# A hybrid decoder step on one core: the last down groups over 148 then 128 columns, the state turned ahead of the squares, a fourth feature place, forget sums in three steps, first queries on GpSimd's queue

## The chip, the core and the metric

The kernel runs on one core of a Trainium2 chip. Its engines are TensorE (PE in the profile; PEld are its weight loads), VectorE (DVE), ScalarE (ACT), GpSimd (POOL) and SyncE (SP); each works through its own instructions in order, and they wait for one another through semaphores. DMAs are issued from the queues of SP, ACT and POOL. The metric is the device time of one execution in microseconds (us).

## The reference

One step of a two-layer decoder over 1,024 prompt rows, 16 meta rows and 64 sample rows (8 requests of 8), 1,024 wide, in fp32. Layer 0 mixes by a recurrence in chunks (8 heads, a state C and a vector n), layer 1 by attention with forget values: 16 heads, scores shifted by cumulative sums of log-forget values. A SwiGLU feed-forward (2,816 wide) follows each.

```
h, state = mlstm_sequence(q, k, v, li, lf, state0, lead)     # layer 0
out = (rmsnorm(h) * sigmoid(og)) @ w_out
...
s = q @ k.T + ci[..., None] - ckT[:, :, None, :]             # layer 1; ci, ckT: cumsum(lf)
p = softmax(where(pos_k <= pi, s, -inf));  o = p @ v
out = (o * sigmoid(og)) @ w_out
...
x = x + (silu(rmsnorm(x) @ w_gate) * (rmsnorm(x) @ w_up)) @ w_down    # after each layer
y = rmsnorm(x) * g_final
```

Outputs are the rows `y`, the states after the step, and the new keys, values and log-forget values.

## The kernel before, in words

An fp32 product is made of three matmuls on parts: each operand is split into a high part (ACT, L255, L261 or L267) and a low part (DVE, L256, L262 or L268), and PE adds high·high, low·high and high·low (L193 to L195, or inside L1402 and L1739). The order of most instructions is set by the framework's scheduler, which also decides which pieces of on-chip memory are used again and so what waits for what; two stretches have PE's order written by hand. The stages, with the places that the change touches:

- **Layer 0, recurrence.** Nine chunks of rows. The 64 sample rows come first: `first_queries` (L1157) stores their queries to DRAM (`qwD`, from POOL) and loads them back in four DMAs into `q2` (L1165, names `qq<-qwD`). Each of the four loads fills one half of the partitions with one of two head groups. DVE copies them into cleared tiles `qms` (L1227; the clearing is POOL's, L1167), and PE multiplies them with the old states (L1232). Each chunk ends with sums of squares of its heads on DVE and ACT (L1258, L1261). After the last chunk `last_state` (L1045) copies the vector n (DVE, L1050, `nnP`), turns it on PE (L1052) and stores it. The output projection `unit` (L517 to L539, PE name `pops`) follows; `add_sq` (L328) keeps the sums of squares for the next norm, its adds on POOL (L347) or, where `late`, on DVE (L345).
- **Feed-forward.** Gate and up products L1402. Down products L1739 run over groups of the weight's rows, for both halves of the outputs in turn. Their feature tiles come from DRAM by POOL's queue (L1529, `hr<-hB…`) into three places, and each is split by ACT and DVE (L267, L268); a split starts the load of the tile three items later. In layer 0 (`each`) the norm of finished column blocks runs beneath the products: sums (L360), root on ACT (L363), a copy on ACT (L379), reciprocal and a diagonal on DVE (L369, L371), and PE spreads it (L378, `nps`).
- **Layer 1, values and forget sums.** Values are projected in column groups 3, 1, 2 (`tmps`). `forget` (L2147 on) turns the log-forget rows on PE (L2169), scans them on DVE (L2174, `cnB`), stores them (`cD`), turns them back on PE (L2178, `fgcq`) and copies them (L2179, `cqP`). Beside it DVE makes the samples' own sums (`ncn`, L2223).
- **Layer 1, attention.** `attend_sample` (PE's order by hand) goes through pages of cached keys and values and, between them, projects the output gates `ogb` (ACT L2139, stored by POOL as `og2D`, L2140). Its last part multiplies sample queries with the new keys; the queries stand in two cleared tiles `qmt`, which live in the pool `sk` and are filled by 16 DVE copies of 64x16 elements. Then `attend_prompt` loads, per pair of heads, queries and keys in high and low parts (SP, L2524: `qh`, `kh`, `kl`, `ql`), the forget sums `ncb` (L2525, 1 MB), the values `vr` (L2531, L2533) and gates (L2537). PE makes scores `sp` (L2605), DVE takes maxima (L2609), POOL subtracts masks (`nd`, L2575).
- **Layer 1, feed-forward and tail.** The second feed-forward ends in class `Tail`: in the last two of the down groups (z = 6, the second half of the outputs, four row blocks of 128, so twelve matmuls of 276 columns for each of four m) each m is added (DVE L1383), squared (ACT L1814) and summed (DVE L1815). PE turns the rows back (L1825), the sums give root and reciprocal (L1846, L1848, L1849), DVE and ACT write the scaled rows (L1860, L1858), and SP stores them in six DMAs (L1863).

Of the kernel before, what the change touches and what calls it, by code (L numbers as in the profile page):

```python
# [176 lines left out]
class Net:  # L177
# [292 lines left out]
    def mlp(self, H, raws, w, l, heads=None, cb=None):  # L470
# [5 lines left out]
        with self.pool(self.uid("nsp")) as sp, self.pool(self.uid("npp"), bufs=2, space=PSUM) as pn:  # L476
# [14 lines left out]
            with ExitStack() as c:  # L491
# [30 lines left out]
                def unit(t, m, x):  # L522
# [9 lines left out]
                    self.add_sq(H, t, m, sp, x, KT - 1 if t < 3 else KT - 3)  # L532
# [424 lines left out]
def recurrence(self, kp, rec, v, qkD, fill, gate):  # L957
# [12 lines left out]
    with ExitStack() as cr, self.pool("recAp", bufs=2, space=PSUM) as pp:  # L970
# [28 lines left out]
        with self.pool("rec2") as sets[2], self.pool("rec1", bufs=2) as rp, self.pool("rec3") as sets[0]:  # L999
# [8 lines left out]
            for i in range(1, NT):  # L1008
# [10 lines left out]
                self.chunk_out(i, R, rp, *args, den, ssq, g, exp=N2 and N2["exp"])  # L1019
                if i == NT - 1:  # L1020
                    self.last_state(C[i % 2], pp, rp)
# [134 lines left out]
@_add(Net)  # L1156
def first_queries(self, R, sp):  # L1157

    nc = self.nc
    qd = self.dram.tile([P, 4, NS], F32, name="qwD")  # L1160
    nc.gpsimd.dma_start(qd, R["qw"][:, :, :NS])
    q2 = R["q2"]
    for a in range(2):
        for z in range(2):
            nc.sync.dma_start(q2[a * 64 : a * 64 + 64, :, z, :], qd[z * 64 : z * 64 + 64])  # L1165
    for qm in R["qms"]:
        nc.gpsimd.memset(qm, 0.0)  # L1167
# [26 lines left out]
def chunk_out(self, i, R, rp, pp, kp, C, v, qkD, eD, wD, tm, den, ssq, f, sp=None, exp=None):  # L1194
# [57 lines left out]
    if exp:  # L1252
        exp()
    R["nps"] = nps
# [99 lines left out]
def ffn(self, H, l, weights, order, TA, pn, pair, each, early, end=None):  # L1354
# [14 lines left out]
    with self.pool(f"ffn{l}") as fp, self.pool(f"ffnp{l}", space=PSUM) as pp:  # L1369
# [3 lines left out]
        fs = [fs0[:, x * SL : x * SL + SL] for x in range(6)]  # L1373
        fs += [H[3][:, k] for k in range(4)] + [H[2][:, k] for k in range(KT)] + [H[3][:, k] for k in range(4, KT)]
# [148 lines left out]
        def h_load(y):  # L1523
            if y < len(items):
# [3 lines left out]
                hraw[y] = self.ny(f"hr{l}_{y}")[:, :m]  # L1528
                nc.gpsimd.dma_start(hraw[y], hB[h, rounds[z][1]][:, c[0] : c[-1] + 1])  # L1529

        def h_split(y):
# [4 lines left out]
            h_load(y + 3)  # L1536
# [83 lines left out]
        with fixed(E.DVE, E.Activation):  # L1620
# [90 lines left out]
            for i, (hs, z, c) in enumerate(seq):  # L1711
# [18 lines left out]
                for m, h in [(m, h) for h in hs for m in range(4)] if apart else [(m, h) for m in range(4) for h in hs]:  # L1730
# [13 lines left out]
                    if last:  # L1744
# [3 lines left out]
                        if z in whole:  # L1748
# [6 lines left out]
                            elif not each and hs == (1,) and z == 6:  # L1755
                                square(3, m)
# [30 lines left out]
            if each:  # L1787
                self.first_values(H, pp, pn, lambda: norm(1, 2))
            else:
                tail.finish()  # L1790


class Tail:


    def __init__(self, net, fp, bank, pn, place):
        self.net, self.fp, self.bank, self.pn = net, fp, bank, pn
# [3 lines left out]
        self.count = {2: 0, 3: 0}  # L1801

    def square(self, t, m):
        nc, H = self.net.nc, self.net.H
        a, b = max(TS[t][0], self.at), TS[t][1]
        src = H[:, m, a:b]
        o = slice(a - self.at, b - self.at)
        c = self.count[t]
        self.count[t] += 1
        if c == 0:  # L1810
            nc.scalar.activation(self.sum[:, o], src, AF.Square)
        else:
            x = self.tmp[c % 2][:, : b - a]
            nc.scalar.activation(x, src, AF.Square)  # L1814
            nc.vector.tensor_tensor(out=self.sum[:, o], in0=self.sum[:, o], in1=x, op=ALU.add)  # L1815

    def gains(self):
        net = self.net
        for k in range(4, KT):
# [3 lines left out]
    def turn(self, ps, x, k):  # L1823
        t0, t1 = TT[DONE[3][x]]
        self.net.nc.tensor.transpose(ps[x][:, k % 4 * P : k % 4 * P + P], self.net.H[:, k, t0:t1], self.net.ident)  # L1825

    def new(self):
        return self.pn.tile([P, 512], F32, name=self.net.uid("fin"), tag="n")

    def second(self):  # L1830
        self.hi = [self.bank("fin"), self.bank("fin"), self.new()]
        for x in range(3):
            for k in range(4, KT):
                self.turn(self.hi, x, k)

    def finish(self):
        net, fp = self.net, self.fp
        nc, O, H = net.nc, net.O, net.H
        gr = net.sq[:, :512]
        lo = [self.bank("fin") for _ in range(3)]  # L1840
        ps = self.new()
        for x, ks in ((0, (0, 1)), (1, (0, 1)), (0, (2,)), (1, (2,)), (2, (0, 1, 2)), (0, (3,))):
            for k in ks:
                self.turn(lo, x, k)
        for x in range(3):
            nc.tensor.matmul(ps[:, x : x + 1], self.sum[:, x * P : x * P + P], net.ones[:, :1], start=True, stop=True)  # L1846
        r = fp.tile([P, 2, 3], F32, name="tr")
        nc.scalar.activation(r[:, 0], ps[:, :3], AF.Sqrt, scale=1.0 / D, bias=net.eps)  # L1848
        nc.vector.reciprocal(r[:, 1], r[:, 0])  # L1849
        for x in (1, 2):  # L1850
            self.turn(lo, x, 3)
        for x, i in enumerate(DONE[3]):
            t0, t1 = TT[i]
            for g, z in enumerate((lo, self.hi)):
                o = H[:, 4 * g : 4 * g + 4, t0:t1]
                y, rr = z[x].rearrange("p (k n) -> p k n", k=4), r[:, 1, x : x + 1]
                if g:
                    nc.scalar.activation(o, y, AF.Copy, scale=rr)  # L1858
                else:
                    nc.vector.scalar_tensor_tensor(out=o, in0=y, scalar=rr, in1=gr.rearrange("p (k n) -> p k n", k=4),  # L1860
                                                   op0=ALU.mult, op1=ALU.mult)
                dst = O["y_prompt"][0, (i - 1) * P : i * P, g * 512 : g * 512 + 512]
                nc.sync.dma_start(dst.rearrange("p (k n) -> p k n", k=4), o)  # L1863
# [131 lines left out]
def phase_b(self, ys, w7, cb):  # L1995
# [11 lines left out]
    with self.pool("fb", bufs=2) as fp, self.pool("fbp", bufs=2, space=PSUM) as pp:  # L2007
# [19 lines left out]
        for c in (3, 1, 2):  # L2027
# [11 lines left out]
            if c == 1:  # L2039
                for _ in forget:  # L2040
                    pass
# [109 lines left out]
def forget(self, lf):  # L2151
    nc, I, O = self.nc, self.I, self.O
    with self.pool("fg") as fp, self.pool("fgp", bufs=1, space=PSUM) as pp:
# [21 lines left out]
        nc.gpsimd.dma_start(self.cD, cn)  # L2175
# [634 lines left out]
```

## Time and profile before

| | |
|---|---|
| median of 3 runs | 2877.62 us (2868.31 to 2879.89) |
| the profiled execution | 2877.98 us |
| span of its instructions | 2876.3 us |
| mean granted TensorE clock | 0.988 |
| PE busy | 2778.6 us, 97% of the span |
| DVE, ACT, POOL busy | 1779.4, 1166.3, 833.7 us |
| DMA, mean | 163 GB/s |

The profiled execution is 1.7 us longer than its span. A row of a timeline shows start, duration, engine, line, operation, out<-in, shapes and count (x), and in brackets how long the engine was idle before and what ended that. A row of the windows view shows, for a stretch, its length, each engine's busy time with its count, the granted clock (1.00 is full), the DMA engines' share and GB/s. A row of the waits view shows total us, number and longest wait.

### The profile page before, as it was taken

Reading aid. Unit: us, or ns where it says so; the run is one execution under the profiler, and the core shown is the slowest. Engines: PE = TensorE matmul, PEld = TensorE weight load, DVE = VectorE, ACT = ScalarE, POOL = GpSimd, SP = SyncE. Lnnn points to the kernel's source line nnn. Section 1 sums busy time; section 2 is a strip of 40 time slices with the busy share of each in tenths; the row PEclk is TensorE's granted clock in tenths of the full one; section 3 lists DMA queues with packets and bytes.
Section 4 is the critical chain, followed back from the end, with each engine's and each line's share of the span. In section 5 each row is a group of like instructions: output and inputs, shape, how many; then the busy total and the mean of one; then the engine's idle time right before and its main releaser. Section 6 shows DMA issues by size and latency. Waiting matters only on the chain. (4 is left out here: it accounts for less than half of the span.)

```text
span 2876.3 us, 60505 instructions
## 1 busy us (share of the span) xinstructions
PE 2778.6 (97%) x23608; PEld 2663.7 (93%) x23608; DVE 1779.4 (62%) x3933; ACT 1166.3 (41%) x2279; POOL 833.7 (29%) x1291
## 2 busy tenths in 40 slices
PE   7999999999999999999999998999999999999998
PEld 7998888999999999999999887777899999999998
DVE  5141566788887656563355542677468888875656
ACT  5232363333232233443344443777533322323345
POOL 3021233223233322124263201455322232332111
PEclk9999999999999999999999998999999999999999
DMA  6374537245555375545343685443424555526566
GB/s 197 104 212 126 144 117 258 80 131 168 176 165 159 104 232 174 188 149 158 131 165 136 221 303 186 152 139 126 146 70 125 175 163 170 166 91 223 184 193 219
DMA packets 429353, 469.45 MB, mean 163 GB/s; under 512 B 41054, under 2 KB 355546, under 8 KB 428042
## 3 DMA queue, kind: packets, MB, share of 16 engines
q1 hardware_dynamic: 380066, 317.04, 35.7%
q0 software_dynamic: 43472, 142.88, 15.1%
q10 hardware_dynamic: 5528, 5.65, 0.6%
q8 instruction: 186, 3.05, 0.4%
q14 instruction: 101, 0.83, 0.1%
HBM read 318.25 MB, written 147.21 MB: 162 GB/s over the span
## 5 line engine op out<-in xcount | busy, mean ns | idle before, releaser
L1402 PE MATMUL m<-xh,slot 128*128 128x276 f32 x2752 | 540.6, 290 | 1.8 <-ACT fs L1431 1.8
L1402 PEld LDWEIGHTS m<-xh,slot 128*128 128x128 f32 x2752 | 439.6, 188 | 3.7 <-ACT fs L1431 2.4
L1402 PE MATMUL m<-xl,slot 128*128 128x276 f32 x1376 | 397.1, 289 | 0.0
L1402 PEld LDWEIGHTS m<-xl,slot 128*128 128x128 f32 x1376 | 258.7, 188 | 0.0
L193 PE MATMUL tmps<-slot,xh 128*128 128x256 f32 (+2 forms) x864 | 243.8, 282 | 0.0
L194 PE MATMUL tmps<-slot,xh 128*128 128x256 f32 (+2 forms) x864 | 241.5, 280 | 0.0
L195 PE MATMUL tmps<-slot,xl 128*128 128x256 f32 (+2 forms) x864 | 241.4, 279 | 0.0
L268 DVE TENSOR_TENSOR slot<-slot,slot 128x1024 fp32r<-128x1024 f32 x124 | 163.0, 1315 | 60.7 <-ACT slot L267 59.0
L267 ACT CAST slot<-slot 128x1024 fp32r<-128x1024 f32 x124 | 129.5, 1045 | 125.4 <-PE m L1402 109.8
L194 PEld LDWEIGHTS tmps<-slot,xh 128*128 128x128 f32 (+1 forms) x864 | 160.0, 185 | 0.2
L195 PEld LDWEIGHTS tmps<-slot,xl 128*128 128x128 f32 (+1 forms) x864 | 159.4, 185 | 0.0
L193 PEld LDWEIGHTS tmps<-slot,xh 128*128 128x128 f32 (+1 forms) x864 | 159.2, 184 | 0.1
L193 PE MATMUL mmA<-xh,whi 128*128 128x384 f32 (+1 forms) x384 | 134.0, 349 | 1.1 <-ACT stg L732 1.0
L194 PE MATMUL mmA<-xl,whi 128*128 128x384 f32 (+1 forms) x384 | 126.9, 330 | 0.0
L195 PE MATMUL mmA<-xh,wlo 128*128 128x384 f32 (+1 forms) x384 | 126.8, 330 | 0.0
L268 DVE TENSOR_TENSOR slot<-vA,slot 128x1024 fp32r<-128x1024 f32 (+1 forms) x59 | 82.2, 1396 | 32.7 <-ACT slot L267 31.5
L268 DVE TENSOR_TENSOR slot<-Ht,slot 128x1024 fp32r<-128x1024 f32 (+1 forms) x59 | 82.0, 1392 | 32.7 <-ACT slot L267 31.6
L256 DVE TENSOR_TENSOR wlo<-wraw,whi 128x1024 fp32r<-128x1024 f32 (+1 forms) x32 | 38.9, 1225 | 101.7 <-ACT whi L255 76.3
L267 ACT CAST slot<-Ht 128x1024 fp32r<-128x1024 f32 (+1 forms) x59 | 60.8, 1036 | 95.6 <-PE m L1402 88.6
L267 ACT CAST slot<-vA 128x1024 fp32r<-128x1024 f32 (+1 forms) x59 | 60.8, 1035 | 95.5 <-PE m L1402 82.7
L1506 DVE TENSOR_TENSOR ws<-ws 128x128 f32<-128x128 f32 x264 | 93.8, 355 | 8.8
L2632 ACT ACTIVATE s<-s,nb 128x272 f32<-128x272 f32 (+7 forms) x126 | 98.9, 787 | 0.0
(770 smaller groups left out, 8699.9 us busy)
## 6 DMA issues: line engine op xcount, KB each, us to landing
ws<-in_w_down SPq DMA_DIRECT2D x176, 128.0 KB
sD<-ws SPq DMA_DIRECT2D x176, 128.0 KB
slot<-sD SPq DMA_DIRECT2D x40, 512.0 KB
slot<-in_w_gate_up SPq DMA_DIRECT2D x36, 512.0 KB
kp<-in_cache_k SPq DMA_DIRECT2D x32, 512.0 KB
vp<-in_cache_v SPq DMA_DIRECT2D x32, 512.0 KB
vA<-in_w_gate_up SPq DMA_DIRECT2D x26, 512.0 KB
Ht<-in_w_gate_up SPq DMA_DIRECT2D x26, 512.0 KB
```

The source lines that it names most:

```text
L193: mm(ps, sh, mh, start=first, stop=False)
L194: mm(ps, sh, ml, start=False, stop=False)
L195: mm(ps, sl, mh, start=False, stop=last)
L256: low = lambda: nc.vector.tensor_tensor(out=lo, in0=raw, in1=hi.bitcast(F32), op=ALU.subtract)
L267: self.nc.scalar.copy(hi, src)
L268: self.nc.vector.tensor_tensor(out=lo, in0=src, in1=hi.bitcast(F32), op=ALU.subtract)
L1402: nc.tensor.matmul(u.ps[h, b], w[p][:, k], x[q][:, k], start=first and k == i == 0, stop=k == 3 and i == 2, skip_group_check=True)
L1506: tt(out=o, in0=a, in1=b, op=ALU.subtract)
L2632: nc.scalar.activation(ss[z, u], ss[z, u], AF.Exp, bias=nb[:, z : z + 1], accum_out=sm[:, u, z : z + 1])
```

## The change

It has seven parts.

1. The third block of the output projection (t = 2, both layers) makes the adds of two sums of squares on DVE and no more on POOL.
2. `last_state` runs between the copies of the last chunk's results and its sums of squares.
3. The four loads of the first queries go through POOL's queue and no more through SP's.
4. In layer 0's down products every fourth feature tile from item 11 on goes to a fourth place, the unused part of the tile `fs0`, and loads are issued four items ahead.
5. `forget` stops once more: turn and scan run at column group 1, the turning back at column group 2.
6. The two `qmt` tiles become one shared name in `attend_sample`'s own pool, cleared and filled by GpSimd (memset and copies). `sk`, which the memory behind comes after, is 4 KB a partition smaller.
7. The last two down groups leave the loop. `finish` makes them per m, first over the 148 columns that hold row tiles 6 and 7, then over the last 128; turning, root, scaling and stores of tiles 6 and 7 stand between the products of the last 128 columns.

```diff
-                    self.add_sq(H, t, m, sp, x, KT - 1 if t < 3 else KT - 3)
+                    self.add_sq(H, t, m, sp, x, KT - 1 if t < 2 else KT - 3)
...
-                if i == NT - 1:
-                    self.last_state(C[i % 2], pp, rp)
+                               then=(lambda: self.last_state(C[i % 2], pp, rp)) if i == NT - 1 else None)
...
-            nc.sync.dma_start(q2[a * 64 : a * 64 + 64, :, z, :], qd[z * 64 : z * 64 + 64])
+            nc.gpsimd.dma_start(q2[a * 64 : a * 64 + 64, :, z, :], qd[z * 64 : z * 64 + 64])
...
+        spare = fs0[:, 1024 : 1024 + 2 * SL].rearrange("p (k n) -> p k n", k=2)
-                hraw[y] = self.ny(f"hr{l}_{y}")[:, :m]
+                hraw[y] = (spare if each and y % 4 == 3 and y > 8 else self.ny(f"hr{l}_{y}"))[:, :m]
-            h_load(y + 3)
+            h_load(y + (4 if each and y > 8 else 3))
+            if each and y == 8:
+                h_load(12)
...
-            if c == 1:
-                for _ in forget:
-                    pass
+            if c != 3:
+                next(forget, None)
...
         nc.gpsimd.dma_start(self.cD, cn)
+        yield
         ps = pp.tile([P, 8, HB], F32, name="fgcq", tag="fg")
...
-    self.qmt = [sp.tile([P, 4, P], F32, name=f"qmt{g}") for g in range(2)]
-    for q in self.qmt:
-        nc.gpsimd.memset(q, 0.0)
...
-        Q = self.qmt[g]
+        Q = sp.tile([P, 4, P], F32, name=f"qmt{g}", tag="qmt")
+        nc.gpsimd.memset(Q, 0.0)
-                nc.vector.tensor_copy(Q[r, j, (2 * j + z) * NM : (2 * j + z + 1) * NM], qt[r, 4 * g + j, NS:])
+                nc.gpsimd.tensor_copy(Q[r, j, (2 * j + z) * NM : (2 * j + z + 1) * NM], qt[r, 4 * g + j, NS:])
...
-            for i, (hs, z, c) in enumerate(seq):
+            for i, (hs, z, c) in enumerate(seq if each else seq[:-2]):
...
+        def product(m, a, b):
+            o = acc[m, 1][:, a - c0 : b - c0]
+            todo = [(p[:, k, m * P : m * P + P], q[:, k, a - c0 : b - c0]) for (wh, wl), (ah, al) in groups
+                    for k in range(wh.shape[1]) for p, q in ((wh, ah), (wh, al), (wl, ah))]
+            for j, (p, q) in enumerate(todo):
+                nc.tensor.matmul(o, p, q, start=False, stop=j == len(todo) - 1, skip_group_check=True)
+            nc.vector.tensor_tensor(out=H[:, m, a:b], in0=H[:, m, a:b], in1=o, op=ALU.add)
+            return self.square(3, m, a, b, keep=b == c2 and m == 3)
+
+        for m in range(4):
+            product(m, c0, c1)
+        product(0, c1, c2)
+        lo = [self.pn.tile([P, 512], F32, name=net.uid("fin"), tag="n") for _ in range(2)]
+        for k in range(4):
+            for ps, i in zip(lo, DONE[3]):
+                self.turn(ps, i, k)
+        sums = [acc[m, 1][:, 508:511] for m in (0, 3)]
+        whole = [(self.sum, 0)]
+        self.inverse((0, 1), sums[0], whole)
+        product(1, c1, c2)
+        self.out(0, lo[0], self.hi[0])
+        hi = self.bank("fin")
+        for k in range(4, KT):
+            self.turn(hi, DONE[3][2], k)
+        product(2, c1, c2)
+        self.out(1, lo[1], self.hi[1])
+        last = product(3, c1, c2)
+        lo = self.bank("fin")
+        for k in range(4):
+            self.turn(lo, DONE[3][2], k)
+        self.inverse((2,), sums[1], whole + [(last, c1 - self.at)])
+        self.out(2, lo, hi)
```

`inverse` makes the sums, root and reciprocal of the row tiles named, `out` scales one row tile on DVE and ACT and issues its two stores.

How the order moves at three places. First POOL's own instructions around the first queries, before (`qq` are the queries' tiles, `C` the state, `qk`, `eb`, `wb` the next chunk's inputs, `ogD` a store of gates):

```order
L1161 DMA qwD<-wb_3020 512x1x64
L1167 MEMSET qq 128x400 x2
L1189 TENSOR_TENSOR C_111<-C_109,wcP 128x516
L1073 DMA qk_3186<-qkD 128x8x128
L1072 DMA eb_3026<-eD 128x8x128
```

and now:

```order
L1160 DMA qwD<-wb_3020 512x1x64
L1164 DMA qq<-qwD 64x4x64 x4
L1166 MEMSET qq 128x400 x2
L1188 TENSOR_TENSOR C_111<-C_109,wcP 128x516
L1072 DMA qk_3186<-qkD 128x8x128
L1071 DMA eb_3026<-eD 128x8x128
```

The four loads now stand behind the store on POOL, and ahead of the clearing and of the next chunk's loads.

Second, DVE around the forget sums, before (`slot` rows are splits of weights for the next projections, four columns of k each):

```order
L2223 TENSOR_TENSOR ncn<-cnew,rowm 128x8 x8
L2174 SCALAR_TENSOR_TENSOR cnB<-onB,ltB 16x1040
L2179 COPY cqP<-fgcq 128x128
L262 SCALAR_TENSOR_TENSOR slot_4933<-slot_4927,gain,slot_4929 128x256 x4
L262 SCALAR_TENSOR_TENSOR slot_4934<-slot_4926,gain,slot_4930 128x256 x4
```

and now:

```order
L2262 TENSOR_TENSOR ncn<-cnew,rowm 128x8 x8
L2212 SCALAR_TENSOR_TENSOR cnB<-onB,ltB 16x1040
L262 SCALAR_TENSOR_TENSOR slot_4933<-slot_4927,gain,slot_4929 128x256 x4
L262 SCALAR_TENSOR_TENSOR slot_4934<-slot_4926,gain,slot_4930 128x256 x2
L2218 COPY cqP<-fgcq 128x128
L262 SCALAR_TENSOR_TENSOR slot_4934<-slot_4926,gain,slot_4930 128x256 x2
```

The copy of the turned sums, and with it PE's turning `fgcq`, has moved behind six of the eight splits for the projection after next; on PE the turning stands 188 matmuls later than before.

Third, SP's queue from the samples' meta values (`vmS`) to the first head pair of the prompt, with the semaphores that each load waits for (DMASW lanes are POOL's DMAs, DMAHW lanes SP's and ACT's), before:

```order
L2426 DMA vmS<-vD 16x1024 [waits DMAHW1_49,DMASW4_49,PE_49]
L2524 DMA qh_20381<-qDh 128x1040 [waits DMASW5_49,DMASW3_49,DMASW6_49,DMASW2_49,DMASW7_49,DMASW1_49,DMAHW2_49,DMASW0_49,Activation_49]
L2524 DMA kh_20388<-kDh 128x1040 [waits DMAHW3_49]
L2524 DMA kl_20389<-kDl 128x1040 [waits DMAHW4_49]
L2524 DMA ql_20390<-qDl 128x1040 [waits DMAHW5_49]
L2525 DMA ncb_20393<-cD 128x2080 [waits DMAHW6_49]
```

and now:

```order
L2462 DMA vmS<-vD 16x1024 [waits DMAHW5_49,DMASW0_49,PE_49]
L2561 DMA qh_20362<-qDh 128x1040 [waits DMAHW6_49]
L2561 DMA kh_20369<-kDh 128x1040 [waits DMAHW7_49,Activation_49]
L2561 DMA kl_20370<-kDl 128x1040 [waits DMAHW0_49]
L2561 DMA ql_20371<-qDl 128x1040 [waits DMAHW1_49]
L2562 DMA ncb_20374<-cD 128x2080 [waits DMAHW2_49]
```

The order is the same; `qh` no longer waits for POOL's stores nor for ACT, and `kh` waits for an instruction of ACT, a split of gate weights (L261).

More of the change, by code (lines that the diff above doesn't have):

```diff
@@ L1253, in chunk_out @@
         exp()
+    if then:
+        then()
     R["nps"] = nps
@@ L1830, in second @@
     def second(self):
-        self.hi = [self.bank("fin"), self.bank("fin"), self.new()]
-        for x in range(3):
+        self.hi = [self.bank("fin"), self.bank("fin")]
+        for ps, i in zip(self.hi, DONE[3]):
             for k in range(4, KT):
[L1834 to L1863, printed above, removed]
```

79 lines of the change are left out of this document (54 added, 25 removed).

## The prediction

> **What bounds the kernel now.** I read the profile's slices first, then PE's waits by releaser, then the windows view at each long wait.
>
> ```profile
> PE 2778.6 (97%) x23608; PEld 2663.7 (93%) x23608; DVE 1779.4 (62%) x3933; ACT 1166.3 (41%) x2279; POOL 833.7 (29%) x1291
> PEclk9999999999999999999999998999999999999999
> ```
>
> PE is busy for 97% of the span, so what PE loses is almost all that can be won without removing products: some 98 us of idleness, and the stretches in which its clock is low. The waits view names the single places:
>
> ```profile
> PE sp L2605 <- DMA kh<-kDh: 7.2, 1, 7.2
> PE fgcq L2178 <- DVE cnB L2174: 6.7, 1, 6.7
> ...
> PE nps L378 <- DVE sq L371: 5.4, 1, 5.4
> PE nps L1232 <- issue: 4.9, 1, 4.9
> ...
> PE nnpP L1052 <- DVE nnP L1050: 3.1, 1, 3.1
> ```
>
> These are single waits, and each of the five stands at a place that the diff touches. Each also has a second price, which the windows view shows:
>
> ```profile
> 268.80:273.30 4.50, 4.43 (x20) 4.44 (x21) 0.34 (x2) 0.00 (x0) 0.00 (x0) 0.50 0.44 112
> 445.00:450.80 5.80, 5.75 (x26) 5.75 (x27) 4.63 (x8) 1.32 (x2) 1.65 (x3) 0.50 0.80 272
> 1211.00:1215.40 4.40, 4.31 (x17) 4.09 (x18) 1.65 (x2) 2.45 (x4) 0.05 (x1) 0.50 0.26 73
> 1367.50:1372.40 4.90, 4.86 (x26) 4.83 (x27) 0.29 (x1) 0.00 (x0) 2.63 (x5) 0.50 0.73 261
> 1372.40:1377.30 4.90, 4.90 (x45) 4.90 (x45) 0.00 (x0) 0.75 (x2) 0.00 (x0) 1.00 0.02 3
> 1783.60:1795.70 12.10, 8.72 (x32) 6.98 (x34) 2.25 (x16) 2.19 (x5) 4.85 (x10) 0.50 0.95 354
> ```
>
> After each wait PE works at a granted clock of 0.50 for 4 to 12 us. In 4.9 us it ends 26 matmuls at half clock and 45 of the same kind at full clock: what is done in such a stretch would take about 0.55 of its time. So a wait that goes also gives back some 0.45 of the cold stretch behind it, if the rest of the wait is short enough to leave the clock up.
>
> **The change part by part**, against the profiled 2877.98 us (0.01% above the median of the runs, so the same forecast serves both).
>
> *First queries.*
>
> ```profile
> qwD<-wb POOLq DMA_DIRECT2D x1, 128.0 KB, 2.3
> ...
> 258.48 0.74 POOL L1161 DMA_DIRECT2D qwD<-wb  x1 [0.44 <-DVE wb L1153]
> ...
> 260.85 3.33 SPq L1165 DMA_DIRECT2D qq<-qwD  x4
> ...
> 263.63 0.17 DVE L1227 COPY qq<-qq 64x32 f32<-64x32 f32 x1 [3.32 <-DMA qq<-qwD]
> 268.59 0.59 DVE L1227 COPY qq<-qq 64x32 f32<-64x32 f32 x3 [4.78 <-DMA qq<-qwD]
> ```
>
> DVE's copies wait for the third of the four loads, until 268.59, and PE with them. The store lands at 258.48 + 2.3 = 260.8; then POOL issues four loads at 0.74 or a little less, the third ends its issue near 263 and, at the store's 2.3 us less its issue, lands near 265. Nothing of the next chunk runs beside it, since its loads now stand behind. The clearing follows at about 264.5. PE resumes near 265.5 instead of 268.9, 3.3 us, and the half-clock stretch gives 0.45 x 4.4 = 2.0; I take **-4.8** for a late landing. Bounds: 0, if the third load lands as late as now, and -7, if nothing is waited for. The next chunk's loads go 3 us later; their cover is the samples' own chunk, through which PE still has to go, and no wait of PE on them is in the list.
>
> The Trainium skill ("DMA: Bandwidth & Descriptors", Specifications) speaks against this part: a first byte takes about 1 us on GpSimd's path and 0.6 us on SP's. As an estimate from it the term would be -4.4 instead of -4.8; no view here shows when SP's loads land.
>
> *Last state.*
>
> ```profile
> 443.14 0.56 DVE L268 TENSOR_TENSOR xl<-ogqk,xh 128x384 fp32r<-128x384 f32 x1
> ...
> 444.83 0.16 DVE L1050 COPY nnP<-C 128x4 f32<-128x4 f32 x1
> ```
>
> The copy comes right after the split at 443.14, so at about 443.6 instead of 444.83: -1.2. The projection behind it needs that split too, so no more. Cold time: between 0 and 0.45 x 3.4; I take 0.3, together **-1.5** (0 to -3). The sums of squares are some 0.7 us later; they feed a norm for which PE has a whole projection to do.
>
> *Fourth place.*
>
> ```profile
> 1203.96 0.42 ACT L267 CAST T0A_1h<-hr 128x276 fp32r<-128x276 f32 x1
> 1209.32 0.42 ACT L267 CAST T0A_1h<-hr 128x276 fp32r<-128x276 f32 x1 [4.94 <-DMA hr<-hB_1T]
> ...
> 1204.62 0.54 POOL L1529 DMA_DIRECT2D hr<-hB_1T  x1 [16.22 <-DVE T0B_2l L268]
> ...
> 1205.49 0.44 DVE L268 TENSOR_TENSOR T0A_1l<-hr,T0A_1h 128x276 fp32r<-128x276 f32 x1
> 1209.78 0.45 DVE L268 TENSOR_TENSOR T0A_1l<-hr,T0A_1h 128x276 fp32r<-128x276 f32 x1 [3.85 <-ACT T0A_1h L267]
> 1210.50 0.44 DVE L371 TENSOR_TENSOR sq<-ident,sq 92x276 f32<-92x276 f32 x1
> ```
>
> Here a cast stands ahead of the norm's steps on ACT and waits 4.9 us for a tile whose load waited 16 us for a place. With one place more it is issued before that pause, so it has long landed. The cast goes at 1204.4; DVE, busy until 1205.93 with the split before (1205.49 + 0.44), makes its part then instead of at 1209.78; the diagonal follows 3.85 earlier, and PE. Cold: 0.45 x 4.3 = 1.9, since the rest of the wait is 1.5 us. **-5.7** (-2 to -6.5). Elsewhere in this phase PE has no such wait.
>
> *Forget sums.*
>
> ```profile
> 1357.85 0.48 DVE L262 SCALAR_TENSOR_TENSOR slot<-slot,gain,slot 128x256 fp32r<-128x256 f32 x1 [0.51 <-ACT slot L261]
> ...
> 1365.18 2.31 DVE L2174 TENSOR_TENSOR_SCAN cnB<-onB,ltB 16x1040 f32<-16x1040 f32 x1
> ```
>
> The weights of the next column group are split by 1358.3, so PE can start it at 1367.5 - 6.7 = 1360.8 and turns the sums 188 products of 4.9/45 us, 20 us, later, long after the scan's end at 1367.5. The whole 6.7 goes, and 0.45 x 4.9 = 2.2: **-8.8** (-6 to -10). What is late next would be the two splits now behind `cqP`; they end about a microsecond before PE needs them.
>
> *Attention's start.*
>
> ```profile
> SPq L2524 <- DMA og2D<-ogb: 15.5, 1, 15.5
> ...
> 1762.52 0.33 SPq L2426 DMA_DIRECT2D vmS<-vD  x1
> 1780.47 0.43 SPq L2525 DMA_DIRECT2D ncb<-cD  x1
> ...
> 1776.33 0.58 POOL L2140 DMA_DIRECT2D og2D<-ogb  x1 [1.60 <-ACT ogb L2139]
> ...
> 1790.52 0.72 POOL L2575 TENSOR_TENSOR nd<-ncb,mneg 128x256 f32<-128x256 f32 x1 [13.39 <-DMA ncb<-cD]
> ...
> 1763.00:1776.50 13.50, 13.03 (x84) 11.97 (x83) 3.20 (x16) 7.37 (x11) 2.49 (x9) 1.00 0.10 33
> ```
>
> This is the largest term, and the diff doesn't name it. SP stands 15.5 us at `qh` until the last gate store, issued 1776.33, has landed, because the loads go into memory that held gates. `ncb`, issued 1780.47, is used at 1790.52. With `sk` smaller the memory is another, and none of the five loads waits for these stores (the order's waits). They follow `vmS` from 1762.9, 15.8 us earlier, into a stretch where the DMA engines are 0.10 busy, and so land by about 1775. PE's products before it end at 1776.5. What PE did cold by 1795.7, 8.7 us of work, is some 4.8 at full clock: it would be there at 1781.3 instead of 1795.7, 14.4. POOL's `nd` now waits for nothing but its store and ends its first four (0.7 each) by 1780; I take **-14** (-8 if `ncb` comes 6 us late, -16). GpSimd's clearing and eight copies between the two halves of the samples' attention take about 2 us beside PE's gate projections, under 0.5 us of risk.
>
> *Tail.*
>
> ```profile
> 2855.41 1.47 PE L1825 MATMUL fin<-ident,Ht 128*128 128x128 f32 x12
> 2856.64 0.37 PE L1739 MATMUL dps<-T1B_4h,slot 128*128 128x276 f32 x1
> ...
> 2862.69 0.29 PE L1739 MATMUL dps<-T1B_4h,slot 128*128 128x276 f32 x1
> ...
> 2867.70 2.07 DVE L1860 SCALAR_TENSOR_TENSOR Ht<-fin,tr,sq 128x512 f32<-128x512 f32 x3
> ...
> 2868.34 4.13 SPq L1863 DMA_DIRECT2D out_y_prompt<-Ht  x6
> ```
>
> Now 48 matmuls of 276 columns take 6.2 us (0.129 each). Twelve turnings of 128 columns come at (2855.41 to 2856.64)/12 = 0.10 to 0.11 each, the nearest row for 128 or 148 columns: 96 take some 10.5, so PE ends 4.3 later, near 2868.2 with the turnings between. Behind that stands only one row tile: add, square, sums, root and reciprocal about 1.7, one scaling of 0.7 in place of three, two stores of 0.69 in place of six: issued by 2872.0 instead of 2872.5, with fewer in flight. **-1** (+2, if narrow products cost 0.12, to -3).
>
> *Squares.* Two adds of 128x276 a layer, some 0.44 each as the row at 1205.49, come to DVE, where it is busy: **+0.6** for both layers (-1 to +1.5).
>
> Sum: -4.8 - 1.5 - 5.7 - 8.8 - 14 - 1 + 0.6 = -35.2, so 2877.98 - 35.2 = 2842.8, **2843 us**.
>
> On the clock: of the first wait's 4.8 us (264.0 to 268.8), the grant averages 0.76, so the half came after some 2.5 us.
>
> ```profile
> 264.00:268.80 4.80, 0.01 (x1) 0.00 (x0) 0.18 (x2) 0.00 (x0) 2.25 (x4) 0.76 0.97 239
> ```
>
> The Trainium skill ("TensorE: Matmul & The Clock Gate", Part 1) has the half clock after at least one idle window of about 3.4 us that runs freely. The trace differs: 2.5 us sufficed. By that rule the remaining waits of about 1.5 us would be free of it; by the trace one that shares a window with others could still cost 2 us, which the range holds.
>
> **The rivals.**
>
> *The early loads don't come early.* Nothing in the diff's words speaks of them; if they still queue until the stores have landed, the 14 stays: 2857. For it: the gain hangs on where memory is placed. Against it: the waits as built.
>
> *The next wait takes the place.* Each stage has another engine close behind: the next feature tile's cast, the copies of the next query group, POOL's `nd`. If half of each of the five gains is waited for there, 17 come back: 2860. Against it: at each place the next inputs were ready microseconds before PE.
>
> *Slower: the fourth place shares its tile with a weight slot.* `fs0` also holds weights in its first 1,024 columns. If loads of one half waited for the other half's split, each of the 19 tiles from item 11 to 83 could meet such a wait. The one late tile of the row at 1209.32 cost PE 5.4; at half of it 19 x 2.7 = 51, so 2843 + 51 = 2894. It decides from 35/19 = 1.9 us a tile on. Against it: as built each such load waits for the split of its own half only.
>
> **How the numbers follow.** Forecast 2843, chance 0.77, own range 2832 to 2853; late loads at 2857, 0.11; next waits near 2860 (2855 to 2868), 0.08; slower 0.04. 0.5% is 14.4 us, about what a measurement of this kernel can tell from no change; that is 2863.2. Faster holds the forecast, the first rival and about half of the second, 0.92; same 0.04; slower 0.04. For 8 in 10 the range goes from 2831 to 2860.
>
> **What would show it.** Right: no PE wait over 2 us at L1232, L378, L2178 and L2605's first product; SP issues `qh` within 2 us of `vmS`; the clock stays at 1.00 there; PE's last product ends about 8 us before the span does. Wrong: a wait on `ncb` or `nd` at attention's start, a wait on a feature tile in layer 0's down products, or DVE late for the splits behind `cqP`.

## The result, and the profile after

| | before | after |
|---|---|---|
| median of 5 runs each (us) | 2872.59 (2868.31 to 2879.89) | 2852.91 (2845.93 to 2854.73) |
| ratio, 95% | | 0.9924 [0.9902, 0.9946] |
| profiled execution (us), its span | 2877.98, 2876.3 | 2854.73, 2853.0 |

The change makes the kernel faster by 0.76%, some 20 us of the 35 that were forecast; the time lies within the forecast's own range of 2832 to 2853, at its very end. More runs put the kernel before near 2872.6, so its profiled execution was 5 us above the middle.

The page of the changed kernel, its span, busy times and granted clock:

```profile
span 2853.0 us, 60631 instructions
PE 2787.0 (98%) x23658; PEld 2675.0 (94%) x23658; DVE 1772.2 (62%) x3929; ACT 1168.6 (41%) x2284; POOL 831.5 (29%) x1307
PEclk9999999999999999999999999999999999999998
```

PE's busy time rose by 8.4 us while the span fell by 23.3. The split last products are 48 matmuls more; but a busy PE also counts slow matmuls in full, and the clock row now ends in an 8. PE's waits at the places of the change, by releaser (us in total, times, longest):

```profile
PE nnpP L1051 <- DVE nnP L1049: 1.9, 1, 1.9
PE nps L1231 <- POOL C L1188: 1.8, 1, 1.8
...
PE nps L378 <- DVE sq L371: 1.3, 1, 1.3
...
PE dps L1876 <- DVE T1B_4l L268: 1.0, 1, 1.0
```

The forget sums and `kh` are gone from the list. The first queries' wait is down to 1.8 and has another cause, POOL's update of the state. The last row is new: in the last down products PE waits 1.0 us for a split.

The next table says where the time went: the same matmul is looked up in both traces and its start compared, so each row is what PE gained (-) or lost in that stretch of the program (limits by the first profile of before).

| stretch | forecast | after | the same kernel again | other kernels |
|---|---|---|---|---|
| 0 to 255, code unchanged | 0 | +5.0 | -0.6 | -1.1 to +3.5 in eleven profiles |
| 255 to 300, first queries | -4.8 | -3.5 | -5.2 | SP still loading them: -4.4, -5.8, -5.9 |
| 432 to 460, last state | -1.5 | -2.4 | -2.4 | part left out: -0.3, -1.2 |
| 520 to 560, squares, layer 0 | +0.3 | -0.8 | -0.9 | part left out: 0.0, +1.5 |
| 1150 to 1230, fourth place | -5.7 | -6.0 | -6.0 | part left out: -0.3, +0.1 |
| 1340 to 1395, forget sums | -8.8 | -9.0 | -8.8 | part left out: 0.0, +0.2 |
| 1750 to 1830, attention's start | -14 | -13.2 | -14.6 | 4 KB more in a pool: +0.7 |
| 2840 to the end, tail | -1 | **+10.6** | **+12.7** | part left out: +0.5; narrow without the new wait: +0.1 |

The windows view of the changed kernel's tail (us, then busy time and count of PE, PEld, DVE, ACT, POOL; granted clock; share of the DMA engines; GB/s):

```profile
2822.00:2825.30 3.30, 2.03 (x13) 1.54 (x13) 2.63 (x4) 1.91 (x3) 0.00 (x0) 1.00 0.14 38
2825.30:2828.20 2.90, 2.88 (x24) 2.89 (x24) 0.84 (x3) 0.65 (x2) 0.00 (x0) 0.91 0.00 0
2828.20:2831.60 3.40, 3.40 (x18) 3.40 (x17) 0.53 (x2) 0.33 (x1) 0.00 (x0) 0.50 0.03 7
2831.60:2835.00 3.40, 3.40 (x17) 3.40 (x17) 0.73 (x3) 0.33 (x1) 0.00 (x0) 0.50 0.00 0
2835.00:2840.00 5.00, 5.00 (x25) 5.00 (x25) 0.64 (x4) 0.57 (x2) 0.00 (x0) 0.50 0.00 0
2840.00:2853.00 13.00, 7.28 (x36) 7.05 (x34) 3.54 (x10) 3.03 (x7) 0.00 (x0) 0.50 0.42 121
```

The first row holds a wait of 1.0 us. Some 2.4 us behind it (the second row's mean of 0.91 is half a microsecond at half clock) the clock falls and stays at half to the end. PE is busy for 3.40 of 3.40 us and ends 17 or 18 matmuls in that time, where 24 took 2.9 us just before. The wait itself, in PE's timeline:

```profile
2823.00 0.32 PE L1876 MATMUL dps<-T1B_4h,slot 128*128 128x148 f32 x1
...
2825.32 0.34 PE L1876 MATMUL dps<-T1B_4l,slot 128*128 128x148 f32 x1 [1.01 <-DVE T1B_4l L268]
```

and what it waits for, in DVE's:

```profile
2824.53 0.73 DVE L268 TENSOR_TENSOR T1B_4l<-hr,T1B_4h 128x552 fp32r<-128x552 f32 x1
```

This `T1B_4l` is an input of the second of the last two groups. In the old order the 24 products of the first group came ahead of it and one of the second; the new `product(0, ...)` runs both groups for its row block at once and so needs that split after 7 products.

### The profile page after: what moved, and what is told of

It is laid out like the page before. It is cut to its first block, busy times and chain, and to the rows that moved or that the text cites. A ratio compares the mean times of both kernels' runs of the same rounds, so it can differ in the third digit from the quotient of the medians.

```text
span 2853.0 us, 60631 instructions
## 1 busy us (share of the span) xinstructions
PE 2787.0 (98%) x23658; PEld 2675.0 (94%) x23658; DVE 1772.2 (62%) x3929; ACT 1168.6 (41%) x2284; POOL 831.5 (29%) x1307
## 4 chain that ended last, share of the span: by engine, by line
PE 81%; DVE 6%; issue 5%; ACT 3%; DMA 2%; POOL 2%; SPq 1%; DVEq 0%; POOLq 0%; ACTq 0%
PE m L1404 30%; PE dps L1743 16%; PE tmps L195 4%; PE tmps L194 4%; PE tmps L193 4%; PE pops L193 2%; PE pops L195 2%; PE pops L194 2%; PE sp L2642 2%; PE op L2729 1%; DVE s L2646 1%; PE mmA L193 1%; PE tp L2696 1%; PE ktp L2353 1%; PE bps L193 1%
```

## The experiments

Theories on the tail. **A**: narrow products (148 and 128 columns) take the clock down by themselves. **B**: the wait of 1.0 us does, whatever the width. **C**: it takes both, and narrow products don't bring the clock up again.

**The old tail.** The kernel after with `finish` and the loop over the groups as before.

```diff
-            for i, (hs, z, c) in enumerate(seq if each else seq[:-2]):
+            for i, (hs, z, c) in enumerate(seq):
...
```

> The changed kernel with the tail of before (part 7 undone, the other six kept). In the changed kernel's profile the tail is 10 us longer than before: the clock is granted at 0.50 from 2828 us to the end. Theory A (narrow products): products of 148 and 128 columns, each with a weight of its own, keep PE busy but let the clock fall. Theory B (the wait): the wait of 1.0 us for the feature split at 2825.3 drops the clock and chance keeps it low. Both expect here a clock of 1.00 up to the last product and a span 9 to 11 us shorter than the changed kernel's 2853.0, 2842 to 2844, so that the six other parts are worth 32 to 34 us together.

Measured: 2843.50 us (2841.43 to 2843.78), 0.9897 [0.988, 0.9913] of before's 2872.86. The six other parts are worth 29 us (32 to 34 were expected, from the long first profile of before), and the tail's part takes 8 or 9 of them away again (changed kernel: 2852.91, and 2851.66 in a later run).

**A wide tail.** The new tail with 276 columns in each product, with the first group ahead where its second isn't ready, and with all three row tiles finished behind the last product.

```diff
-        for m in range(4):
-            product(m, c0, c1)
-        product(0, c1, c2)
+        for m, g in ((0, 0), (1, 0), (2, 0), (0, 1), (1, 1), (3, 0), (2, 1), (3, 1)):
+            product(m, g)
...
```

> The changed kernel with a third tail: the last two groups are again taken per row block, but over all 276 columns, in the order of the groups 0 0 0 1 1 0 1 1 so that no product waits for the second group's split; all three row tiles are then finished together. Theory A: wide products, so the clock stays at 1.00 to the last of 48 products at 0.129 us; adds and squares begin earlier than in the old tail, which saves about 1 us: span 2841 to 2843. Theory B gives the same here. If the clock halves in spite of the wide products, A is wrong.

Measured: 2839.87 us (2837.97 to 2842.74), 0.9884 [0.9868, 0.9901]; no wait on `T1B_4l`, clock 1.00 until the products are done. This alone leaves A, B and C standing, since both suspects are gone.

**Narrow, without the wait.** The changed kernel, but the first group for all four row blocks ahead of the second.

```diff
...
         for m in range(4):
-            product(m, c0, c1)
+            product(m, c0, c1, (0,))
+        for m in range(4):
+            product(m, c0, c1, (1,))
```

> The changed kernel with the first 48 narrow products in another order: the first group for all four row blocks, then the second, so that the second group's split (ready 1.7 us after the first group's start in the changed kernel) is waited for no more. Theory A: no wait of PE in the narrow products, and yet the clock falls to 0.50 within 4 to 8 us of their start; span within 2 us of 2853. Theory B: the clock stays at 1.00, 96 narrow products take 10.6 us at 0.11, span 2843 to 2845.

Measured: one run, 2846.32 us; the tail at +0.1 instead of +10.6, no wait on `T1B_4l`, no fall of the clock in the products. The same kernel timed over six runs:

> The narrow tail without its wait once more, now timed. Theory C (a wait sets the fall off, narrow products keep the clock down): again no fall before the last product, and a median 6 to 10 us below the changed kernel's (2851.7 and 2852.9), 2843 to 2846. If the first profile without a fall was chance, this profile falls or the median stays above 2849.

Measured: 2842.42 us (2839.33 to 2844.61), 0.9894 [0.9879, 0.991], the tail again at +0.1. Its windows over the first narrow products:

```profile
2819.70:2823.00 3.30, 3.30 (x32) 3.30 (x31) 1.48 (x4) 0.65 (x2) 0.00 (x0) 1.00 0.00 0
2823.00:2827.00 4.00, 4.00 (x39) 4.00 (x38) 1.74 (x7) 1.23 (x5) 0.00 (x0) 1.00 0.02 6
```

The same matmuls as in the changed kernel, now at full clock: those that start in the first window do so 0.112 us apart. (The count of a window also takes in matmuls that reach into it or out of it.) A falls.

**Narrow products in the old loop.** The kernel before, with each matmul of its last two groups cut into 148 and 128 columns.

```diff
-                            nc.tensor.matmul(o, p[:, k, ms], q[:, k], start=fresh and k == x == 0,
-                                             stop=last and k == nk - 1 and x == 2, skip_group_check=True)
+                            for u, v in ((0, 148), (148, SL)) if not each and i > len(seq) - 3 else ((0, SL),):
+                                nc.tensor.matmul(o[:, u:v], p[:, k, ms], q[:, k, u:v], start=fresh and k == x == 0,
+                                                 stop=last and k == nk - 1 and x == 2, skip_group_check=True)
```

> The kernel of before, in which only the matmuls of the last two down groups are made over 148 and 128 columns (two in place of each, same order, same tail behind). Theory A: the clock falls to 0.50 within 4 to 8 us of the first narrow product, and the span grows by 8 to 13 us against before (2884 to 2889 beside 2876.3). Theory B: there is no wait at that place, the clock stays at 1.00, and the span grows by the 48 further products alone, 96 x 0.11 - 48 x 0.129 = 4.4 us (2880 to 2881).

Measured: one run, 2873.06 us, the tail 2.95 us longer than before's. Its window:

```profile
2849.00:2852.40 3.40, 3.40 (x33) 3.40 (x32) 1.17 (x2) 0.00 (x0) 0.00 (x0) 1.00 0.00 0
```

Again 0.112 us from start to start, at 1.00. That is the price of the narrow products by themselves: some 3 us to the end of the span, and A falls a second time.

**The changed kernel again**, unaltered.

> The changed kernel itself, for a second profile of its tail. Narrow products without a wait kept the full clock in two kernels (the one with the first group taken for all four row blocks first, and the one of before with only the columns split), so theory A as it stood has fallen, and the wait of 1.0 us is what sets it off. Theory B (the wait alone, then chance): the clock may or may not be low in this profile, and if low it can come back during the narrow products. Theory C (both): the wait lets a window of the clock's count fall short, and narrow products at half clock cannot bring it up again, so that once it has fallen it stays at 0.50 to the end: 25 us, span 10 us longer than with the wait removed. C allows a profile without the fall, by where the windows lie, but none with a fall and a recovery within the narrow products.

Measured: 2851.66 us (2846.44 to 2853.03), 0.9918 [0.9897, 0.9938]. In these traces the clock changes only in steps of 3.41 us: ahead of the tail the changed kernel's stretches at half clock are 3.41, 6.83 and 10.24 us long. The first row is the step that ends with the fall:

```profile
2817.86:2821.28 3.42, 2.33 (x16) 1.61 (x14) 2.80 (x5) 2.21 (x4) 0.00 (x0) 1.00 0.22 63
2821.30:2824.70 3.40, 3.22 (x15) 3.23 (x16) 0.43 (x2) 0.33 (x1) 0.00 (x0) 0.50 0.00 0
2824.70:2841.00 16.30, 16.30 (x80) 16.30 (x79) 3.42 (x12) 2.44 (x7) 0.00 (x0) 0.50 0.05 13
```

The step with the wait in it has PE busy for 2.33 us (2.40 in the first profile, 2824.26 to 2827.67). The next one begins at half clock, and 80 matmuls in 16.3 us, started 0.211 us apart without a gap, don't bring it back.

**The wait, with wide products.** The wide tail in the order that runs both groups for each row block.

```diff
-        for m, g in ((0, 0), (1, 0), (2, 0), (0, 1), (1, 1), (3, 0), (2, 1), (3, 1)):
+        for m, g in ((0, 0), (0, 1), (1, 0), (1, 1), (2, 0), (2, 1), (3, 0), (3, 1)):
```

> The third tail (276 columns, per row block) with the two groups taken together for each row block, as the changed kernel does, so that PE waits some 1 us for the second group's split, but with wide products. Theory B: the clock falls as in the changed kernel and stays low as long, 5 to 7 us lost. Theory C: it doesn't fall, or falls and is back at 1.00 within two windows of 3.4 us, before the last product; from the start of the first of the 48 products to the end of the span at most 3 us more than in the kernel with the same tail and no wait.

Measured: one run, 2838.82 us, a wait of 0.95 us, no fall. Taken again:

> The wide tail with its wait once more, now timed. Theory C: no fall that lasts to the end, median within 2 us of the wide tail without a wait (2839.9). Theory B (the wait alone): in some executions the fall comes, median above 2843.

Measured: 2841.91 us (2840.09 to 2845.22), 0.9896 [0.9876, 0.9916]. PE's wait in its last 38 us, and the windows by the steps of its clock:

```profile
PE dps L1876 <- DVE T1B_4l L268: 0.9, 1, 0.9
```

```profile
2817.43:2820.85 3.42, 2.43 (x16) 1.63 (x13) 2.80 (x5) 2.16 (x4) 0.00 (x0) 1.00 0.20 56
2820.85:2824.26 3.41, 3.28 (x25) 3.28 (x26) 1.32 (x4) 0.77 (x2) 0.00 (x0) 1.00 0.00 0
```

This is the closest pair to the changed kernel: the same wait, products of 276 columns instead of 148, and the clock stays. The busy time of the step is a little longer (2.43 us, and 2.46 in the single run, against 2.33 and 2.40). By itself that could part them, but other places speak against it. In the changed kernel's layer 0 (L378) PE waits 1.3 us among products of 276 columns, and with 2.07 us busy the clock stays (first two rows). In the profile of the next experiment the wait at that place is 1.7 us; there the clock falls for one step, and the products of 276 columns bring it back (the other rows):

```profile
1202.93:1206.34 3.41, 2.07 (x15) 1.80 (x14) 2.01 (x6) 0.76 (x4) 1.96 (x4) 1.00 1.04 315
1206.34:1209.76 3.42, 3.42 (x29) 3.42 (x28) 1.87 (x2) 1.88 (x3) 0.28 (x1) 1.00 0.94 362
```

```profile
1197.00:1200.41 3.41, 1.72 (x12) 1.45 (x12) 2.07 (x6) 0.41 (x2) 2.01 (x4) 1.00 0.98 299
1200.41:1203.82 3.41, 3.41 (x17) 3.41 (x16) 1.87 (x2) 2.12 (x4) 0.00 (x0) 0.50 1.00 371
1203.82:1207.23 3.41, 3.41 (x29) 3.41 (x29) 2.78 (x5) 1.81 (x3) 1.08 (x2) 1.00 0.85 265
```

So B falls, and C fits the tail: both profiles with a wait and narrow products fell and stayed down, none of the five in which one of the two was missing did (narrow alone 3, wide with the wait 2). The times agree: seven of the nine executions of the changed kernel took 2850.86 us or more, the kernels with a new tail that lack the wait or the narrow products 2838 to 2847.

As a rule for other places C isn't shown. Late in layer 0's recurrence there are products of 129 columns and fewer, with a wait of 1.0 us among them (L1243). In the changed kernel the clock falls behind it, and the next such products bring it back within one step (first three rows). In the kernel with the wide tail the same wait, with the same 2.06 us busy, leaves the clock up (last two rows):

```profile
424.69:428.10 3.41, 2.06 (x18) 1.34 (x17) 2.68 (x8) 1.17 (x4) 2.07 (x3) 1.00 0.25 50
428.10:431.51 3.41, 3.41 (x20) 2.95 (x20) 1.72 (x5) 1.21 (x4) 1.30 (x4) 0.50 0.85 256
431.51:434.93 3.42, 3.42 (x39) 2.77 (x37) 2.27 (x11) 2.21 (x10) 0.87 (x2) 1.00 1.03 409
```

```profile
420.24:423.65 3.41, 2.06 (x20) 1.46 (x18) 2.33 (x8) 1.49 (x4) 2.11 (x3) 1.00 0.19 21
423.65:427.06 3.41, 2.88 (x35) 2.23 (x33) 1.57 (x5) 1.12 (x3) 1.68 (x4) 1.00 0.94 287
```

What parts these products from the tail's, no run here shows.

**The first queries on SP again.** The old tail, and the four loads back on SP's queue.

```diff
-            nc.gpsimd.dma_start(q2[a * 64 : a * 64 + 64, :, z, :], qd[z * 64 : z * 64 + 64])
+            nc.sync.dma_start(q2[a * 64 : a * 64 + 64, :, z, :], qd[z * 64 : z * 64 + 64])
```

> The changed kernel with the tail of before and the first queries' four loads back on SP's queue (part 3 undone). In the changed kernel PE waits 1.8 us at that place, for POOL's product C, which stands behind the four loads and the clearing. My prediction: the wait of 4.9 us with half clock comes back, +3.5 to +5 against the kernel with the old tail (2843 to 2845 in the span beside 2839.7). Rival: the 4.9 us of the first profile was a long case (a profile of the unchanged code in the kernel with narrow columns alone shows 1.2 us and no fall of the clock); then this kernel is as fast as with the loads on POOL's queue, or up to 2 us faster.

Measured: 2844.58 us (2840.82 to 2846.49), 0.9899 [0.9878, 0.9919], against 0.9897 with the loads on GpSimd. PE's wait there was 2.7 us. The part is worth nothing that can be measured.

**The kernel before, a second profile**, to see how long that wait usually is.

> The kernel of before, for a second profile. If the wait of 4.9 us for the first queries, which my largest but two term rests on, is usual, it comes again with half clock behind it. If it was a long case, it is between 1 and 3 us as in the two other profiles with these loads on SP's queue (1.2 and 2.7), and the span is some 4 us shorter than 2876.3 for this alone.

Measured: 2872.39 us, and of PE's waits from 250 to 300:

```profile
PE nps L1232 <- issue: 1.2, 1, 1.2
```

The 4.9 us of the first profile was a long case: with the loads on SP the wait was 4.9, 1.2, 1.2 and 2.7 in four profiles. On GpSimd's queue it's 1.8 whenever it was looked at; POOL's row shows why:

```profile
263.49 0.74 POOL L1160 DMA_DIRECT2D qwD<-wb  x1 [0.44 <-DVE wb L1152]
266.40 2.48 POOL L1164 DMA_DIRECT2D qq<-qwD  x4 [2.17 <-DMA qwD<-wb]
268.86 0.82 POOL L1166 MEMSET qq<- 128x400 f32 x2
269.63 1.07 POOL L1188 TENSOR_TENSOR C<-C,wcP 128x516 f32<-128x516 f32 x1
```

POOL stands 2.2 us until its own store has landed, then 2.5 us issuing loads, then clears, and only then updates `C`, which PE needs.

**The clearing ahead of the loads**, so that it fills POOL's wait (with the wide tail).

```diff
+    for qm in R["qms"]:
+        nc.gpsimd.memset(qm, 0.0)
...
-    for qm in R["qms"]:
-        nc.gpsimd.memset(qm, 0.0)
```

(ahead of the four loads instead of behind them)

> The kernel with the wide third tail and no wait, and with the clearing of the queries' tiles ahead of their four loads on POOL's queue, where POOL waits for the store anyway. If PE's wait of 1.83 us at that place is the queue on POOL (loads, clearing of 0.9, product C of 1.06), it shrinks to 0.9 us and the stretch from 255 to 300 us is 0.9 us shorter than in the kernels whose clock stayed up there. If the loads themselves end the wait, nothing changes. Median 1 us below the wide tail's, 2837 to 2841.

Measured: 2841.64 us (2839.44 to 2842.72), 0.9885 [0.9868, 0.9903]; the wait falls from 1.8 to 1.3 us, still on `C`. Half a microsecond of the span can't be told in the time: without the edit it was 0.9884.

**Four KB more in the pool.** The old tail, with an unused tile in the pool from which `qmt` had been taken. This puts the memory behind it back to other places without giving POOL any work but one small clearing.

```diff
+    pad = sp.tile([P, 8, P], F32, name="pad")
+    nc.gpsimd.memset(pad[:, 0, :1], 0.0)
```

> The changed kernel with the tail of before and a tile of 4 KB a partition put into the pool that the two cleared tiles left; only one column of it is cleared, and nothing uses it. Clearing and copies of the sample queries stay on GpSimd. If the gain at attention's start comes from where the memory behind lies, the wait of SP on the gate stores comes back, 7 us of waiting on the first keys and about 13 to 15 us in all against the kernel with the old tail (span 2853 to 2855 beside 2839.7). If it comes from the copies that left DVE, or from an earlier end of the samples' part, the span stays within 2 us of 2839.7.

Measured: one run, 2855.78 us. SP's queue, and PE's first wait behind it:

```profile
1739.74 0.33 SPq L2429 DMA_DIRECT2D vmS<-vD  x1
1756.26 0.34 SPq L2528 DMA_DIRECT2D qh<-qDh  x1
```

```profile
PE sp L2609 <- DMA kh<-kDh: 7.3, 1, 7.3
```

The stall of 16.5 us on SP is back, and with it the wait of 7.3 us and 17.1 us of half clock; attention's start is at +0.7 where every other kernel with the part has -13.2 to -14.7. The gain there comes from where the tiles lie; the copies on GpSimd, which this kernel keeps, don't bring it.

## Why the prediction was right and where it failed

*The bound*, PE and what it loses in waits and at half clock, holds: every stretch that moved is one of the two.

*Last state*, *fourth place*, *forget sums*: right in mechanism and size (-2.4, -6.0, -9.0 against -1.5, -5.7, -8.8), each with the wait named gone or cut to 1.3 or 1.9 us, and with full clock behind the last two. The size of the first is one draw's: its wait is 1.9 us in all eleven profiles with the part, but its stretch goes from -0.2 to -3.1, by how much half clock lies around it. The fourth place gave -6.0 in ten of the eleven and -4.2 where the clock fell at L378.

*Attention's start*: right. SP's queue in the changed kernel:

```profile
1744.22 0.33 SPq L2462 DMA_DIRECT2D vmS<-vD  x1
1744.60 0.42 SPq L2561 DMA_DIRECT2D qh<-qDh  x1
...
1746.49 0.49 SPq L2562 DMA_DIRECT2D ncb<-cD  x1
```

`ncb` follows `vmS` by 2.3 us where it was 18, and POOL's `nd` runs at 1759.03 without a wait. The first rival, that the early loads don't come early, is thus refuted. The padded kernel is this rival made real: its span is 14.3 us longer than without the pad (2854.0 against 2839.7), where the rival said 14. The sign "the clock stays at 1.00 there" held in one of the changed kernel's two profiles; in the other one step at half clock begins at 1759.30, which fits -13.2 beside -14.6. The second rival, that the next wait takes half of each gain, came true at the first queries alone, where POOL's update of `C` is waited for. The rival of a shared tile, 51 us slower, didn't occur: layer 0's down products lost nothing.

*Squares*: the sign was wrong. "Two adds of 128x276 a layer, some 0.44 each" was right, 0.43; but the price left out POOL's share, and a wait of PE that hung on it. That wait before:

```profile
PE nps L360 <- ACT sq L339: 0.9, 1, 0.9
```

DVE before:

```profile
526.49 1.95 DVE L104 TENSOR_TENSOR vA<-vA,t 128x552 f32<-128x552 f32 x2
...
529.93 1.88 DVE L104 TENSOR_TENSOR xl<-vA,xh 128x1104 fp32r<-128x1104 f32 x1
```

POOL before, at the same time:

```profile
525.95 1.26 POOL L347 TENSOR_TENSOR sq<-sq 128x276 f32<-128x276 f32 x1 [2.19 <-ACT sq L339]
```

and DVE after:

```profile
525.44 1.36 DVE L104 TENSOR_TENSOR vA<-vA,t 128x552 f32<-128x552 f32 x2
...
527.08 0.43 DVE L345 TENSOR_TENSOR sq<-sq 128x276 f32<-128x276 f32 x1
...
528.66 1.30 DVE L104 TENSOR_TENSOR xl<-vA,xh 128x1104 fp32r<-128x1104 f32 x1
```

DVE's subtraction takes 1.88 us beside POOL's add and 1.30 without, and the pair before it 1.95 and 1.36. The two adds on DVE cost 0.86 and give back 1.17. PE's wait for ACT's squares is gone, in layer 1 too (1.0 us before), and PE is 0.8 us earlier behind layer 0 and some 0.6 behind layer 1. That the two engines slow each other is read from the rows of one place; it wasn't tried by itself.

*First queries*: the time of the working was right, its base was not. PE came back 7.4 us after the store's issue, where the working says 7.0, though what it waits for at last is POOL's update of `C`, which the working doesn't name. Behind it one step at half clock came in the first profile and none in the second (-3.5 and -5.2). But "DVE's copies wait for the third of the four loads, until 268.59" was one execution's long wait, taken as the usual one. Against the usual 1.2 to 2.7 us, 1.8 is no gain: the term is about 0 (by single profiles between 2.4 lost and 0.8 won), not -4.8.

*Tail*: this term failed, "96 take some 10.5, so PE ends 4.3 later". It gives the products 0.11 each, which is the price at full clock and without a wait; the kernels without the wait have that (0.112), and their tail is +0.1 where -1 was forecast. What it didn't look at is the order across the groups. The order, not the width, asks for `T1B_4l` 18 products earlier, and DVE has it 1.0 us late. The prediction asked for each moved step what is late next, but of the tail only what stands behind the products. With the narrow width the clock fell behind this wait and stayed down. Its price by the trace: 1.0 us, and from 2828.2 on 3.40 + 3.40 + 5.00 + 7.28 = 19.1 us of busy PE at 0.50, half of which full clock would save, 9.5; together 10.5, as measured (+10.6 against +0.1). The prediction's own remark on the clock (2.5 us of idleness sufficed, and a wait of about 1.5 us could cost 2) pointed the right way and set the price too low: a wait of 1.0 us cost some 10 here.

*The sum.* Against the usual time of before (2872.59): last state -2.4, squares -1.4, fourth place -6.0, forget -9.0, attention -13.2 to -14.6, tail +10.6 to +12.7 make -21; the medians say -19.7, and -23.8 in the second set of runs (2875.44 to 2851.66). So the other parts of the forecast came in, and the 10 us missing are the tail's 11.6; that the first queries gave nothing didn't show in the absolute time, since the first profile of before, on which it was built, was itself 5 us long. That these two errors cancelled is luck.

*Open*: what the clock's gate counts. Of the nine executions of the changed kernel two were profiled, and both fell; two others (2845.93 and 2846.44 us) took some 6 us less than the rest. The second of these has a mean clock of 0.994, like kernels that didn't fall, where the rest have 0.989 to 0.992, so it may be one without the fall; no profile shows it. Nor is it shown from what length a wait among narrow products does harm, or why the narrow products of layer 0's recurrence bring the clock back and the tail's don't.

*Versions.* The wide tail (0.9884 [0.9868, 0.9901]), narrow without the wait (0.9894) and the old tail (0.9897) all beat both kernels, and can't be told from each other. A new tail gives nothing here that can be measured; the work is in not losing the clock.

## What to carry to other kernels

When the loops around a product are turned over (all groups for one row block instead of all row blocks for one group), look up for each input when its producer ends: the first block needs the last group's inputs earlier by all the blocks that used to come first. In this tail a wait of 1 us cost little among products of 276 columns and ten times as much among those of 148 and 128, so a late wait is better put among wide products. And before a wait's length is written into a sum, see it in a second execution: one profile shows one draw.

## What the runs showed of the hardware

A matmul of 128 or 148 columns doesn't cost what its columns say. At full clock those of 148 columns started 0.112 us apart, those of 276 columns 0.127; at half clock the narrow ones started 0.213 apart, with PE's loads of weights busy all the time too (16.30 of 16.30 us). So narrow products fill PE's busy time while they move few columns: by these figures 1,300 a us at full clock against 2,200.

The granted clock isn't a matter of PE's busy time alone, as the profile gives it (the ends of matmuls in it are modelled): it stayed at half through 16.30 us with PE busy for 16.30, and at full with 2.07 of 3.41 us busy. Nor is it one of the width alone: 20 products of at most 129 columns raised it within 3.41 us in layer 0. The Trainium skill ("TensorE: Matmul & The Clock Gate", Part 1) has full clock after one busy window of about 3.4 us and half after an idle one. These rows differ on both: some five busy windows in a row didn't raise it, and one with 2.33 of 3.42 us busy lowered it.

An unused tile of 4 KB in one pool cost some 14 us in another stage: `qh` then waits on SP's queue for `og2D<-ogb`, GpSimd's last store of gates from the memory that it takes, as it did before the change, and the whole queue stands with it.
